# Second mixture of experts: routing work spread over eleven rounds of first products instead of one, with its data in a pool of its own

## The chip, the cores and the metric

The kernel runs on one core of a Trainium2 chip. The time is the device time of one execution in microseconds (us). TensorE (PE in the profile) multiplies matrices, its weight loads are listed as PEld; VectorE is DVE, ScalarE is ACT, GpSimd is POOL, and SyncE (SP) issues most of the DMA transfers. Each engine works through its own list of instructions in order.

## The reference, cut to what matters

The program is a stack of blocks over x of 256 tokens by 1024 columns in fp32. The part that is changed is the feed-forward stage of the second block of the second network (the "second mixture"): a mixture of 8 experts, of which each token takes two, with d_ff 2816.

```python
def moe_swiglu(x, router_w, router_b, w1, w3, w2):
    logits = (x @ router_w + router_b).astype(jnp.float32)
    top_v, top_i = lax.top_k(logits, TOP_K)          # TOP_K = 2
    top_p = jax.nn.softmax(top_v, axis=-1)
    gate = jnp.sum(jax.nn.one_hot(top_i, N_EXPERTS_2, dtype=jnp.float32) * top_p[..., None], axis=-2)
    out = jnp.zeros_like(x)
    for e in range(N_EXPERTS_2):                     # 8
        out = out + gate[..., e:e + 1] * swiglu(x, w1[e], w3[e], w2[e])
    return out
```

Around it stand an RMS norm of x before (its gain is g_ffn), the addition of the result to x, and afterwards a gated projection and a last norm.

## The kernel before, in words

**Stages.** The program runs through the phases b1, moe1, mix0, ffn0, ple0, mix1, ffn1, ple1 and fin. The second mixture is ffn1, and lies between about 1400 and 2105 us.

**Weights.** All weights of the mixture come as 264 blocks of 1 MB (128 x 2048 fp32), fetched by one queue on SP (class `Stream`, line 236; the transfer is issued in line 264). It has nine slots in this phase, three that all phases share and six more. A slot is given back when the next block is asked for (`get`), so SP waits until the products that read it are done, then issues the next transfer, strictly in the order of use.

**Blocks.** The 8 experts go in two groups c of four. A group has eleven rounds j of first products (gate and up columns), each of 8 blocks (k, one for each 128 of the 1024 columns), so 88 blocks, and then two down products d of 22 blocks. `tiles` (line 1918) does one block: eight products on quarters of the PE array (32 columns each, printed 128*32, tiles u = 0 to 7), whose weights are gathered tokens and which go to PSUM banks r0 and r1; three copies by ScalarE of a part of the block, chosen at run time, into `fw` (line 314, two buffers, FLEX = 2; these are called flex copies here); and six narrower products from `fw` into the third bank. After the 8 blocks of a round, the hand-over: ScalarE takes Silu of the three banks (line 303, `ft<-ps`), VectorE multiplies into `ft`, and, during block 2 of the next round (`flush` at k == 2), transposes `ft` into `hT` (line 2093), the input of the down products. Blocks are counted here from 0 through the whole phase: round j starts at block 8j, and the second group at block 132.

**Routing.** A token's place within its expert turns into a one-hot matrix P (tokens x slots), per group 640 columns: 256 "base" columns, 64 slots for each of the four experts (`base`), and 384 "strip" columns, 12 strips of 32 for the experts with more tokens (`fewest` finds which have the fewest, `strips` spreads the places by six copies into px, `more` compares them with a ramp). From P come:

- the gathers (`gathered`, line 1069): 8 steps per group, one for each 128 columns, four full-width products each (ps<-P,htmh and ps<-P,html, 352 columns); even steps are evicted into xg by VectorE, odd ones by ScalarE;
- the slot sums (`of_slots`, line 1088): one-column products ps<-rs,P that give each slot its token's norm factor (rsl), which Silu and the product after it use as scale;
- the shares (`shares`, line 958): Wt, the two gates of a token, by Exp on ScalarE, then `strips` of it;
- twelve rounds of transposes of P into pt (ps<-c,P, line 233; two or three at a time) with four sets of five share products (ps<-c,Pw) whose sums become wsl; pt and wsl are used after the down products;
- the flag (`over_flag`): whether an expert has more tokens than slots.

**Order.** The order of TensorE, ScalarE and VectorE is that in which the program writes the instructions. The generator `rest()` holds all routing of the second group and what follows; `beside` puts it in a list and each `tick` runs it to its next `yield`; `drain` runs it to its end. In the kernel before, `during(k)` stands ahead of each of the 8 blocks of the first round: two further steps of the first gather, the slot sums at k == 2, `rest()` from k == 3 on with three ticks per block; `drain` follows. The pool m2r that holds P, the places and so on is closed after that round, and m2e (hT, yf, four ft buffers) opens in its place; xs, the overflow's input, is a view of a part of hT that is not yet filled.

**Overflow test.** After round 5 of the first group all engines read the flag (`values_load` of fi) and branch; with these inputs no expert overflows and the branch only skips. The changed lines are 1936 to 2130.

Of the kernel before, what the change touches and what calls it, by code (L numbers as in the profile page):

```python
# [7 lines left out]
F32 = mybir.dt.float32  # L8
F32R = mybir.dt.float32r
# [3 lines left out]
ALU = mybir.AluOpType  # L13
# [3 lines left out]
D, S = 1024, 256  # L17
# [8 lines left out]
CAP1, CAP2 = 32, 64  # L26
# [251 lines left out]
class Kern:  # L278
# [1615 lines left out]
    def moe2(self, x):  # L1894
# [13 lines left out]
        with tc.tile_pool(reuse_waits="tile", name="m2", bufs=1) as pool:  # L1908
# [27 lines left out]
            with tc.tile_pool(reuse_waits="tile", name="m2r", bufs=1) as rt:  # L1936
# [30 lines left out]
                def strips(src, name):  # L1967

                    s, o = four(src), rt.tile([128, 2, 2, 3, 4], F32, name=name)
                    d = rt.tile([128, 2, 2, 3], F32, name=name + "d")  # L1970
                    nc.vector.tensor_sub(d, s[:, :, :, 1:4], s[:, :, :, 0:3])
                    nc.vector.tensor_tensor(d, d, mk[:, None].to_broadcast([128, 2, 2, 3]), op=ALU.mult)
                    nc.vector.tensor_add(d, d, s[:, :, :, 0:3])
                    for i in range(3):
                        n = 3 - i
                        nc.vector.tensor_copy(o[:, :, :, i, :n], d[:, :, :, :n])
                        nc.vector.tensor_copy(o[:, :, :, i, n:], d[:, :, :, n - 1:])
                    return o.rearrange("p t c i g -> p t c (i g)")
# [9 lines left out]
                def rest():  # L1988
                    with self.after((nc.cur_bb, self.first)):
                        base(1)  # L1990
                    more(1)
# [3 lines left out]
                    wx = strips(Wt, "wx")  # L1995
                    bw = self.bank()
                    for t in range(2):
                        for c in range(2):
                            for r0, r1 in ((0, 3), (3, 5)):
                                b = self.bank()  # L2000
                                for r in range(r0, r1):
# [5 lines left out]
                            Pw = rt.tile([128, L], F32, name="Pw")  # L2007
                            Pc = P[:, t, L * c:L * c + L].bitcast(F32)
                            nc.vector.tensor_tensor(v3(Pw[:, :B], CAP2), v3(Pc[:, :B], CAP2), bc(Wt[:, t, 4 * c:4 * c + 4], CAP2),
                                                    op=ALU.mult)  # L2010
                            nc.vector.tensor_tensor(v3(Pw[:, B:], 32), v3(Pc[:, B:], 32), bc(wx[:, t, c], 32), op=ALU.mult)
                            for r in range(5):
                                bw.mm(bw.t[:, 5 * c + r:5 * c + r + 1], Pw[:, 128 * r:128 * r + 128], self.cst("ones")[:, 0:1])
# [35 lines left out]
            m13 = self.A["m13"].rearrange("q j k p e d -> q j k p e d")  # L2049
            m2 = self.A["m2"].rearrange("q f (j c) p e d -> q f j c p e d", c=2)  # L2050

            def units(first, unit):
                with tc.For_i(0, 2, 1) as q:
                    first()
                    with tc.For_i(0, 11, 1) as j:
                        for e in range(4):
                            unit((q, j, e), e)
            one = lambda i: bass.ds(i, 1)
            with tc.tile_pool(reuse_waits="tile", name="m2e", bufs=1) as work:
                hT = work.tile([128, 22, R], F32, name="hT")  # L2060
                yf = [work.tile([128, 512], F32R, name="yf" + n) for n in "hl"]
                for y in yf:
                    nc.vector.tensor_scalar(y, iota[:, None, :].to_broadcast([128, 4, 128]), 0.0, None, op0=ALU.mult)

                xs = hT[:, 16:].rearrange("p a r -> p (a r)")[:, :8 * S].rearrange("p (k s) -> p k s", k=8)
                later = []

                def flush():
                    while later:
                        later.pop(0)()  # L2070

                for c in range(2):
                    for j in range(11):
                        g = g0 if c == j == 0 else first_products(c, lambda k: flush() if k == 2 else None)
                        ts = []
                        for r in range(3):
                            t = work.tile([128, 256], F32, name="ft", bufs=4)
# [19 lines left out]
                        if c == 0 and j == 5:  # L2097
# [3 lines left out]
                                          lambda v: v.rearrange("p (q a i d) -> p q a i d", q=4, a=2, i=2))  # L2101
                    if c:

                        self.raw = self.parts = self.split(F32R)
                    for d in range(2):
# [6 lines left out]
                        ys = [[work.tile([128, 512], F32R, name="y" + n, bufs=2) for n in "hl"] for _ in range(2)] + [yf]  # L2112
# [60 lines left out]
```

## Time and profile before

| What | Value |
|---|---|
| Time, median of 3 runs | 2163.77 us (2163.45 to 2166.29) |
| Profiled execution | 2167.51 us, with a span of 2165.9 us |
| Mean granted clock of PE | 0.976 of full speed |
| PE busy | 2016.7 us, 93% |
| PEld busy | 1461.7 us, 67% |
| VectorE busy | 1060.6 us, 49% |
| ScalarE busy | 1080.2 us, 50% |
| GpSimd busy | 18.7 us, 1% |
| DMA | 613.73 MB, mean 283 GB/s |

The profiled execution is one run, recorded by the hardware; the span goes from its first to its last instruction. Busy time is the time in which an instruction of the engine was under way; weight loads of PE overlap with its products. In the timelines a row is one instruction or a row of like ones (xcount), with the time at which the first began, and in brackets how long the engine idled before and what ended that.

### The profile page before, as it was taken

The page shows a single profiled execution, that of the slowest core. Times are in us where ns is not written, and L with a number is a line of the kernel's source. Part 1 is how long each engine was busy: PE and PEld are TensorE (multiplying, and loading weights), DVE is VectorE, ACT ScalarE, POOL GpSimd, SP SyncE. Part 2 cuts the span into 40 slices and gives each one's busy share as a digit, 9 for nine tenths or more (in the row PEclk, how much of TensorE's full clock was granted, in tenths as well). Part 3 has the DMA queues.
Part 4 walks back from the last instruction along what each step waited for, and adds up shares of the span by engine and source line. Part 5 has one row for each costly group of instructions (what it writes and reads, how often), then busy time and mean ns, then how long its engine had stood idle before and what let it go on. Part 6 is the DMA issues. An engine that isn't in the chain of part 4 may idle for free. (4 is left out here: it accounts for less than half of the span.)

```text
span 2165.9 us, 44126 instructions
## 1 busy us (share of the span) xinstructions
PE 2016.7 (93%) x17740; PEld 1461.7 (67%) x17740; DVE 1060.6 (49%) x2809; ACT 1080.2 (50%) x2178; POOL 18.7 (1%) x29
## 2 busy tenths in 40 slices
PE   7999998787877779999999999999899999999997
PEld 6999994222222248879999888866566756666746
DVE  5787653100100037777666787536655115566115
ACT  5566642000000025456456735457677777777775
POOL 0000000000000010000000100000000000000000
PEclk9999999899999999999999999889999999999998
DMA  5344597999999983316555331449999999999981
GB/s 179 120 146 149 175 376 305 418 420 420 419 420 420 419 343 109 109 61 216 179 193 191 114 128 52 175 159 396 399 410 418 416 405 407 418 418 417 418 351 47
DMA packets 88665, 613.73 MB, mean 283 GB/s; under 512 B 9879, under 2 KB 12071, under 8 KB 18560
## 3 DMA queue, kind: packets, MB, share of 16 engines
q1 hardware_dynamic: 86272, 604.74, 71.1%
q0 software_dynamic: 1344, 5.10, 0.7%
q8 instruction: 143, 2.34, 0.4%
q10 hardware_dynamic: 832, 0.94, 0.1%
q14 instruction: 74, 0.61, 0.1%
HBM read 609.69 MB, written 1.05 MB: 282 GB/s over the span
## 5 line engine op out<-in xcount | busy, mean ns | idle before, releaser
L314 ACT COPY fw<-w 128x512 f32 x792 | 439.0, 617 | 137.3 <-ACT fw L314 91.9
L341 ACT CAST wh<-w 128x512 fp32r<-128x512 f32 (+2 forms) x500 | 289.8, 585 | 293.8 <-PE ps L230 247.1
L342 DVE TENSOR_TENSOR wl<-w,wh 128x512 fp32r<-128x512 f32 (+2 forms) x500 | 317.9, 646 | 169.9 <-ACT wh L341 161.8
L230 PE MATMUL ps<-w,hT 128*32 128x512 f32 x1920 | 311.0, 597 | 31.4 <-DMA w<-wdn 26.0
L230 PE MATMUL ps<-rawh,wh 128*128 128x256 f32 x960 | 277.4, 289 | 1.1 <-ACT rawh L341 1.1
L230 PE MATMUL ps<-rawl,wh 128*128 128x256 f32 x960 | 271.0, 282 | 0.5 <-DVE rawl L342 0.5
L230 PE MATMUL ps<-rawh,wl 128*128 128x256 f32 x960 | 270.5, 282 | 0.0
L230 PE MATMUL ps<-fw,xg 128*32 128x384 f32 (+2 forms) x2112 | 252.8, 382 | 0.0
L230 PE MATMUL ps<-w,xg 128*32 128x512 f32 x1024 | 199.5, 600 | 43.2 <-DMA w<-wgu 43.0
L2093 DVE STREAM_TRANSPOSE hT<-ft 32x64 f32<-32x64 f32 x968 | 228.3, 236 | 16.3 <-DVEq L985 0.7
L230 PE MATMUL ps<-w,rawh 128*32 128x512 f32 x1408 | 206.2, 607 | 6.4 <-issue 6.4
L230 PE MATMUL ps<-w,rawl 128*32 128x512 f32 x1408 | 211.7, 593 | 0.0
L230 PEld LDWEIGHTS ps<-w,hT 128*32 128x32 f32 x1920 | 116.8, 110 | 135.6 <-DMA w<-wdn 64.0
L230 PEld LDWEIGHTS ps<-fw,xg 128*32 128x32 f32 x2112 | 137.8, 110 | 83.0 <-issue 24.0
L230 PEld LDWEIGHTS ps<-rawh,wh 128*128 128x128 f32 x960 | 181.8, 190 | 5.1 <-ACT rawh L341 1.6
L230 PEld LDWEIGHTS ps<-rawl,wh 128*128 128x128 f32 x960 | 181.9, 190 | 1.9 <-DVE rawl L342 0.7
L230 PEld LDWEIGHTS ps<-rawh,wl 128*128 128x128 f32 x960 | 181.9, 189 | 1.5 <-issue 0.9
L230 PEld LDWEIGHTS ps<-w,xg 128*32 128x32 f32 x1024 | 42.1, 109 | 185.7 <-DMA w<-wgu 111.7
L230 PEld LDWEIGHTS ps<-w,rawl 128*32 128x32 f32 x1408 | 105.2, 110 | 34.4 <-issue 0.9
L230 PE MATMUL ps<-hh,wh 128*128 128x256 f32 x416 | 124.4, 300 | 0.1
L230 PE MATMUL ps<-fw,hT 128*32 128x128 f32 (+2 forms) x1056 | 121.1, 380 | 0.5 <-ACT fw L314 0.3
L230 PE MATMUL ps<-hh,wl 128*128 128x256 f32 x416 | 116.2, 281 | 0.2 <-DVE wl L342 0.2
(520 smaller groups left out, 2983.7 us busy)
## 6 DMA issues: line engine op xcount, KB each, us to landing
w<-m SPq DMA_DIRECT2D x264, 1024.0 KB, 10.7
w<-wgu SPq DMA_DIRECT2D x128, 1024.0 KB, 19.9
w<-wdn SPq DMA_DIRECT2D x64, 1024.0 KB, 19.9
w<-f SPq DMA_DIRECT2D x32, 1024.0 KB, 5.1
w<-wz SPq DMA_DIRECT2D x20, 1024.0 KB, 5.5
w<-wdh SPq DMA_DIRECT2D x24, 768.0 KB, 4.3
w<-wb SPq DMA_DIRECT2D x16, 1024.0 KB, 5.6
w<-wo SPq DMA_DIRECT2D x8, 1024.0 KB, 5.1
```

The source lines that it names most:

```text
L230: return self.k.nc.tensor.matmul(out, lhsT, rhs, start=new, stop=stop, skip_group_check=True, **kw)
L314: self.nc.scalar.copy(out, in_)
L341: self.nc.scalar.copy(h, src)
L342: self.nc.vector.tensor_sub(l, src, h.bitcast(F32))
L2093: nc.vector.transpose(hT[32 * f:32 * f + 32, 2 * j:2 * j + 2, o:o + 32], ts[r][32 * s:32 * s + 32, 64 * q:64 * q + 64].rearrange("p (i d) ...
```

## The change: what it does

The routing of the first group keeps its beginning, but with less ahead of the first gather: `strips` is split in two (`thirds`, three VectorE instructions, and `strips`, the six copies), and `more` gets the places and an offset, so that only the first 96 strip columns, one per third, are made before the first gather; the six copies and the other 288 columns are written at k == 5 of the first round. The slot sums of the first group and `rest()` start at k == 7 instead of 2 and 3.

`rest()` then goes on beside the following rounds: `beside(k)` stands ahead of every later block, and steps it once at each odd k, so four times per round, and `yield`s stand between its pieces as before (one more ahead of its gathers). The drain, the closing of the routing's pool and the overflow test follow after round 10 of the first group instead of after round 0 and round 5. For this the routing's pool m2r lies on the other side ("right") of the on-chip memory, hT and ft are in m2e from the start, ft has three buffers instead of four, xs has a pool of its own, yf and ys are in a new pool on the right after the test, and the weighted P (Pw) uses a temporary tile ("rsy") in two pieces. The computation is the same.

```diff
@@ the pools
-            with tc.tile_pool(reuse_waits="tile", name="m2r", bufs=1) as rt:
+            right = lambda name: tc.tile_pool(reuse_waits="tile", name=name, bufs=1, side="right")
+            with ExitStack() as routing, tc.tile_pool(reuse_waits="tile", name="m2e", bufs=1) as work:
+                rt = routing.enter_context(right("m2r"))
...
-                def strips(src, name):
+                def thirds(src, name):
-                    s, o = four(src), rt.tile([128, 2, 2, 3, 4], F32, name=name)
-                    d = rt.tile([128, 2, 2, 3], F32, name=name + "d")
+                    s, d = four(src), rt.tile([128, 2, 2, 3], F32, name=name)
                     nc.vector.tensor_sub(d, s[:, :, :, 1:4], s[:, :, :, 0:3])
                     nc.vector.tensor_tensor(d, d, mk[:, None].to_broadcast([128, 2, 2, 3]), op=ALU.mult)
                     nc.vector.tensor_add(d, d, s[:, :, :, 0:3])
+                    return d
+                def strips(d, name):
+                    o = rt.tile([128, 2, 2, 3, 4], F32, name=name)
...
-                def more(c):
+                def more(c, places, a):
                     for t in range(2):
-                        nc.vector.tensor_tensor(v3(P[:, t, L * c + B:L * c + L], 32), bc(psx[:, t, c], 32),
-                                                iota[:, None, CAP2:CAP2 + 32].to_broadcast([128, 12, 32]), op=ALU.is_equal)
+                        o = v3(P[:, t, L * c + B + a:L * c + B + a + 32 * places.shape[-1]], 32)
+                        nc.vector.tensor_tensor(o, bc(places[:, t, c], 32), iota[:, None, CAP2:CAP2 + 32].to_broadcast(
+                            [128, places.shape[-1], 32]), op=ALU.is_equal)
...
                 def rest():
                     with self.after((nc.cur_bb, self.first)):
                         base(1)
-                    more(1)
+                    more(1, f["px"], 0)
+                    yield
                     yield from gather(1)
...
                 f = {}
+                fewest()
+                pst = thirds(ps, "pd")
                 base(0)
-                fewest()
-                psx = strips(ps, "px")
-                more(0)
+                more(0, pst, 0)
...
                 def during(k):
                     for _ in range(2):
                         next(start, None)
-                    if k == 2:
+                    if k == 5:
+                        f["px"] = strips(pst, "px")
+                        more(0, f["px"][:, :, :, 3:], 96)
+                    if k == 7:
                         self.of_slots(rsl[:, :5], P[:, :, :L], rs)
-                    if k == 3:
                         self.beside(rest(), late=True)
-                    for _ in range(3):
-                        self.tick()
-                g0 = first_products(0, during)
-                self.drain()
...
+                def beside(k):
+                    if k == 2:
+                        flush()
+                    if k % 2:
+                        self.tick()
...
                 for c in range(2):
                     for j in range(11):
-                        g = g0 if c == j == 0 else first_products(c, lambda k: flush() if k == 2 else None)
+                        g = first_products(c, beside if c or j else during)
                         ts = []
                         for r in range(3):
-                            t = work.tile([128, 256], F32, name="ft", bufs=4)
+                            t = work.tile([128, 256], F32, name="ft", bufs=3)
...
-                        if c == 0 and j == 5:
+                    if not c:
+                        self.drain()
+                        routing.close()
+                        with right("m2o") as room:
+                            xs = room.tile([128, 8, S], F32, name="xs")
                             self.overflow(pool, x, ("g_ffn1", xs, lambda: None), rk, *f["over"], E, units,
...
+                        outs = routing.enter_context(right("m2y"))
+                        yf = [outs.tile([128, 512], F32R, name="yf" + n) for n in "hl"]
```

TensorE round the slot sums of the second group, in the kernel before. Here `ps<-P,html` is the last gather product of the group, `ps<-rs,P` a slot sum, `ps<-c,P` a transpose into pt, `w,rawh` and `fw,xg` the products of one block (the latter from the flex copies):

```order
L230 MATMUL ps<-P,html 128x352
L230 MATMUL ps<-rs,P 128x1 x10
L233 MATMUL ps<-c_78,P 128x128 x3
L230 MATMUL ps<-w,rawh 32x512 x8
L230 MATMUL ps<-fw,xg_13969 32x384
L230 MATMUL ps<-fw,xg_13969 32x128
L230 MATMUL ps<-fw,xg_13969 32x256
L230 MATMUL ps<-fw,xg_13969 32x384
L230 MATMUL ps<-fw,xg_13969 32x256
L230 MATMUL ps<-fw,xg_13969 32x128
L233 MATMUL ps<-c_78,P 128x128 x2
```

The gather's last steps, the slot sums, and the transposes come one right behind the other, and the next pieces of the routing follow after each single block. The same place in the changed order, which is now inside the fourth round of first products, after block 27:

```order
L230 MATMUL ps<-fw,xg_13969 32x128
L230 MATMUL ps<-rs,P 128x1 x10
L233 MATMUL ps<-c_78,P 128x128 x3
L230 MATMUL ps<-w,rawh 32x512 x8
L230 MATMUL ps<-fw,xg_13969 32x384
L230 MATMUL ps<-fw,xg_13969 32x128
L230 MATMUL ps<-fw,xg_13969 32x256
L230 MATMUL ps<-fw,xg_13969 32x384
L230 MATMUL ps<-fw,xg_13969 32x256
L230 MATMUL ps<-fw,xg_13969 32x128
L230 MATMUL ps<-w,rawh 32x512 x8
```

The gather's last step now stands two blocks earlier, by itself; the slot sums and three transposes stand between two blocks, and two blocks follow each other before the next piece.

ScalarE in the kernel before, at the end of the first round, with the first Silu (`ft<-ps,rsl`) and the flex copies (`fw<-w`); `pt<-ps` evicts transposes, and ISA belongs to the flex copies, whose source is chosen at run time:

```order
L314 CAST pt<-ps 128x2x128
L314 CAST pt<-ps 128x3x128
L314 CAST pt<-ps 128x2x128
L314 ISA
L314 COPY fw<-w 128x512
L303 ACT_TABLE_LOAD
L303 ACTIVATE ft<-ps,rsl 128x256 x2
L303 ACTIVATE ft<-ps,rsl 128x64
L314 ISA
L314 COPY fw<-w 128x512
```

All casts into pt and the flex copies up to the first hand-over's stand before the first table load; after it only Silu and flex copies follow. ScalarE in the changed order, at a hand-over near the end of the second group's gathers (`rawl<-ps,pv` and `xg<-ps,pv` evict a gather step):

```order
L303 ACTIVATE ft<-ps,rsl 128x64
L314 ISA
L314 COPY fw<-w 128x512
L303 ACTIVATE ft<-ps,rsl 128x64
L295 ACT_TABLE_LOAD
L301 ACTIVATE rawl<-ps,pv 128x256
L301 ACTIVATE xg_13970<-ps,pv 128x96
L314 ISA
L314 COPY fw<-w 128x512
L314 ISA
```

The gather's evictions now stand between Silus and flex copies, with a load of another table before them (line 295, for the Exp of the shares); the casts into pt and the Exp of the shares follow later, between the rounds.

## Rows read from the trace of the kernel before

**Rows 1.** The chain that ended last, shares of the span by engine.
```profile
PE 26%; ACT 1%; DVE 1%; issue 0%; DVEq 0%; ACTq 0%
```

**Rows 2.** Busy us: PE, PEld, DVE, ACT, POOL; granted clock, DMA share, GB/s.
```profile
1409.30:1460.20 50.90, 50.86 (x409) 32.49 (x412) 14.37 (x52) 25.66 (x57) 0.00 (x0) 0.89 0.48 167
1460.20:1550.00 89.80, 89.80 (x1068) 58.66 (x1065) 59.88 (x243) 68.25 (x136) 0.00 (x0) 1.00 0.99 398
```

**Rows 3.** Waits from 1413 to 2106 us: total, number, longest.
```profile
PE ps L230 <- issue: 6.4, 1, 6.4
SPq L264 <- PE ps L230: 598.9, 227, 21.9
```

**Rows 4.** Weight transfers of line 264 between 1460 and 1700 us.
```profile
DMA to landing us min/median/max: 5.2/10.0/15.6
```

**Rows 5.** PE timeline, first products of four blocks: start, us, operation.
```profile
1476.80 0.60 PE L230 MATMUL ps<-w,rawh 128*32 128x512 f32 x1
1479.16 0.60 PE L230 MATMUL ps<-w,rawh 128*32 128x512 f32 x1
1599.65 0.59 PE L230 MATMUL ps<-w,rawh 128*32 128x512 f32 x1
1602.65 0.62 PE L230 MATMUL ps<-w,rawh 128*32 128x512 f32 x1
```

**Rows 6.** Timeline of VectorE and PE before the first gather.
```profile
1408.08 0.15 DVE L1976 COPY px<-pxd 128x12 f32<-128x12 f32 x1
1408.66 1.95 DVE L1982 TENSOR_TENSOR P<-px,c 128x384 fp32r<-128x384 f32 x4
1409.34 0.63 PE L230 MATMUL ps<-P,htmh 128*128 128x352 f32 x1 [3.41 <-DVE P L1982]
```

**Rows 7.** PE timeline, the routing among the first blocks.
```profile
1417.35 1.92 PE L230 MATMUL ps<-w,rawh 128*32 128x512 f32 x16
1419.09 0.83 PE L230 MATMUL ps<-fw,xg 128*32 128x384 f32 x12
1419.85 0.43 PE L230 MATMUL ps<-P,htmh 128*128 128x352 f32 x1
1420.11 0.32 PE L230 MATMUL ps<-P,html 128*128 128x352 f32 x1
1420.27 0.32 PE L230 MATMUL ps<-P,htmh 128*128 128x352 f32 x1
1421.22 2.29 PE L230 MATMUL ps<-rs,P 128*128 128x1 f32 x20
1423.44 3.24 PE L230 MATMUL ps<-w,rawh 128*32 128x512 f32 x16
1426.43 1.27 PE L230 MATMUL ps<-fw,xg 128*32 128x384 f32 x12
...
1441.99 3.08 PE L230 MATMUL ps<-w,rawh 128*32 128x512 f32 x16
```

**Rows 8.** Busy time, the 10 us round the first slot sums.
```profile
1420.00:1430.00 10.00, 10.00 (x71) 7.29 (x72) 2.25 (x7) 4.41 (x11) 0.00 (x0) 0.83 0.51 175
```

**Rows 9.** Timeline of ScalarE and PE's weight loads at hand-overs.
```profile
1457.35 1.28 ACT L303 ACT_TABLE_LOAD   x1
1458.64 1.04 ACT L303 ACTIVATE ft<-ps,rsl 128x256 f32<-128x256 f32 x3
...
1465.86 1.66 ACT L314 COPY fw<-w 128x512 f32 x3 [0.70 <-ACT fw L314]
...
1602.62 0.12 PEld L230 LDWEIGHTS ps<-fw,xg 128*32 128x32 f32 x3 [0.38 <-ACT fw L314]
```

**Rows 10.** PE timeline at the overflow test.
```profile
1559.76 3.64 PE L230 MATMUL ps<-w,rawh 128*32 128x512 f32 x16 [6.44 <-issue]
1564.14 1.91 PE L230 MATMUL ps<-w,rawh 128*32 128x512 f32 x16
```

**Rows 11.** VectorE timeline, the transposes into hT after a hand-over.
```profile
1464.40 7.78 DVE L2093 STREAM_TRANSPOSE hT<-ft 32x64 f32<-32x64 f32 x31
```

More of the change, by code (lines that the diff above doesn't have):

```diff
@@ L1994, in rest @@
                     Wt = self.shares(rt, oh1, oh2, v1, v2, E)
-                    wx = strips(Wt, "wx")
+                    wx = strips(thirds(Wt, "wd"), "wx")
                     bw = self.bank()
@@ L2006, in rest @@
                                 yield
-                            Pw = rt.tile([128, L], F32, name="Pw")
                             Pc = P[:, t, L * c:L * c + L].bitcast(F32)
[L2009 to L2013, printed above, removed]
+                            for r0, n, col in ((0, CAP2, Wt[:, t, 4 * c:4 * c + 4]), (2, 32, wx[:, t, c])):
+                                m = n * col.shape[-1]
+                                Pw = self.tmp.tile([128, 512], F32, name="rsy")[:, :m]
+                                nc.vector.tensor_tensor(v3(Pw, n), v3(Pc[:, 128 * r0:128 * r0 + m], n), bc(col, n), op=ALU.mult)
+                                for r in range(m // 128):
+                                    bw.mm(bw.t[:, 5 * c + r0 + r:5 * c + r0 + r + 1], Pw[:, 128 * r:128 * r + 128],
+                                          self.cst("ones")[:, 0:1])
                             yield
@@ L2040, in during @@
                         next(start, None)
-                    if k == 2:
+                    if k == 5:
+                        f["px"] = strips(pst, "px")
+                        more(0, f["px"][:, :, :, 3:], 96)
+                    if k == 7:
                         self.of_slots(rsl[:, :5], P[:, :, :L], rs)
-                    if k == 3:
                         self.beside(rest(), late=True)
-                    for _ in range(3):
-                        self.tick()
-                g0 = first_products(0, during)
-                self.drain()
[L2049 to L2059, printed above, removed]
                 hT = work.tile([128, 22, R], F32, name="hT")
[L2061 to L2065, printed above, removed]
                 later = []
@@ L2070, in flush, with units @@
                         later.pop(0)()
+                def beside(k):
[3 more added lines that the diff above has]
+                        self.tick()
+                m13 = self.A["m13"]
+                m2 = self.A["m2"].rearrange("q f (j c) p e d -> q f j c p e d", c=2)
+                def units(first, unit):
+                    with tc.For_i(0, 2, 1) as q:
+                        first()
+                        with tc.For_i(0, 11, 1) as j:
+                            for e in range(4):
+                                unit((q, j, e), e)
+                one = lambda i: bass.ds(i, 1)
                 for c in range(2):
                     for j in range(11):
-                        g = g0 if c == j == 0 else first_products(c, lambda k: flush() if k == 2 else None)
+                        g = first_products(c, beside if c or j else during)
                         ts = []
                         for r in range(3):
-                            t = work.tile([128, 256], F32, name="ft", bufs=4)
+                            t = work.tile([128, 256], F32, name="ft", bufs=3)
                             gu = g[r].t.rearrange("p (q a d) -> p q a d", a=2, d=64)
@@ L2101, in moe2 @@
                                           lambda v: v.rearrange("p (q a i d) -> p q a i d", q=4, a=2, i=2))
+                        outs = routing.enter_context(right("m2y"))
+                        yf = [outs.tile([128, 512], F32R, name="yf" + n) for n in "hl"]
+                        for y in yf:
+                            nc.vector.tensor_scalar(y, iota[:, None, :].to_broadcast([128, 4, 128]), 0.0, None, op0=ALU.mult)
                     if c:
@@ L2111, in moe2 @@
                                 flush()
-                        ys = [[work.tile([128, 512], F32R, name="y" + n, bufs=2) for n in "hl"] for _ in range(2)] + [yf]
+                        ys = [[outs.tile([128, 512], F32R, name="y" + n, bufs=2) for n in "hl"] for _ in range(2)] + [yf]
                         for r in range(3):
```

## The prediction

> **What bounds the kernel now.** I read the page first (times by engine, then the chain that ended last), then busy time by stretch, then the waits of TensorE and of the weight queue inside the second mixture, and last the instructions in order of time around its routing.
>
> The page offers two suspects. The chain that ended last is TensorE for 26% of the span, some 560 us, with the other engines at 1% or less [rows 1]: it is followed back to 1560 us, into the second mixture, and lies on TensorE nearly all that way. But the table by stretch shows the DMA share at 0.99 and 398 GB/s there as well (1460 to 1550 us), after a stretch from 1409.3 to 1460.2 us in which DMA is at 0.48 and 167 GB/s [rows 2]. That stretch is the routing: TensorE alternates eight blocks of the first products with gathers, slot sums, transposes and share products. If weights were late, the empty stretch would be worth filling. The waits say who is late: from 1413 to 2106 us TensorE's only long wait is one of 6.4 us with no releaser, and no DMA releases it at all, while the queue that issues weights waits 598.9 us for TensorE [rows 3]. Issue to landing is at most 15.6 us between 1460 and 1700 us [rows 4], and nine slots at 2.36 us a block (1476.80 to 1479.16 [rows 5]) are 21 us. DMA looks full because TensorE frees one slot after another, just about as fast as they can be filled. So in this mixture TensorE's own time sets the end, and moving its work along its in-order queue gains only what it idles or wastes now.
>
> **The change, term by term.** I compare with the profiled execution (2167.51 us), which is 3.74 us above the median 2163.77 of the runs shown.
>
> 1. *Head.* The first gather waits 3.41 us for P [rows 6]. VectorE now makes only 96 of the 384 strip columns first, and the six copies into px come after them. The copies start at 1408.08 and the strips at 1408.66 [rows 6]; one of four strip products is 1.95 / 4 = 0.49, and a quarter as wide I take 0.2. That is 0.4 to 0.6 for the copies and the share product between, 0.3 for the narrower strip: **-0.7** (0 to -0.9). ScalarE now evicts a gather before the first flex copies; those are needed only when the wide products of block 0 are through, so I count nothing.
>
> 2. *Breaks.* Every piece of the routing remains (the same gathers, slot sums, transposes, share products, flag), so their raw times cancel. What changes is how often TensorE leaves the 32-column products for full-width ones. Now the pieces stand in 9 gaps, after blocks 0 to 8; in the new order they stand in 25: after blocks 0, 1, 2 and 6, eight single gathers on every second block, then slot sums with three transposes, eleven gaps of two or three transposes or five share products, and the flag. One gap costs: a block alone takes 2.50 (1417.35 to 1419.85 [rows 7]) against 2.36 in a run [rows 5], 0.13 or so; the first gather product takes 0.26 to its successor (1419.85 to 1420.11) where the next takes 0.16 (to 1420.27), 0.10; and the way back 0.10. So a gather gap has 0.33 of waste, a gap of transposes or share products 0.13 to 0.23. Eight more gather gaps at 0.33 are 2.6; eight other ones at 0.13 are 1.0: **+3.6**. Bounds: 16 x 0.10 = 1.6 and 16 x 0.33 = 5.3.
>
> The rows show the loss at each change of width. [...]
>
> 3. *Half clock.* Both runs of slot sums (ps<-rs,P, 2.2 us of one-column products, 1421.22 to 1423.44) are followed by a block at 3.24 and 3.08 instead of 1.92 [rows 7]; the granted clock is 0.83 in the 10 us round the first [rows 8], where the dense stretch has 1.00 [rows 2]: part of it at 1.2 GHz, the rest at 2.4. The first cost (3.24 + 1.27) - (1.92 + 0.83) = 1.76, the second 1.16, together 2.9. In the new order the slot sums stand alone amid dense blocks. The trace does not show such a place. Both ends: both remain (0), both vanish (-2.9). I take one of two, **-1.4**.
>
> 4. *ScalarE's order.* A block needs three flex copies, 1.66 of each 2.36, so ScalarE has 0.70 to spare [rows 9]. At the hand-over to the next first products its Silus stand among them. Where copies go first nothing is lost (2.36 [rows 5]); where all three copies of a block stand behind the first Silus, TensorE waits for fw and the block starts 3.00 after the one before (1599.65 to 1602.65 [rows 5, 9]): 0.64. That happens now at four hand-overs of the first group, after the overflow test. In the new order the first three are clean, four are late as now (to blocks 56 to 80), two (to 32 and 48) half late, 0.5 each. Also two more ACT_TABLE_LOADs stand there, since the exponential's set is asked for after Silu: 1.28 each [rows 9]. One comes before the last gather eviction and a block's copies, beyond the 0.70: 0.5; the other stands in idle time before a Silu. **+1.5** (0 to +4.2).
>
> 5. *The overflow test* moves from the middle of the first products to their end. It costs 6.44 idle and a first block that takes 4.38 instead of 2.36 (1559.76 to 1564.14 [rows 10]), 8.5. TensorE idles although nothing holds it, so I let it cost the same at the new place: **0** (-0.6, as it swallows a late hand-over, to +0.8). Its flag stands after block 49 in the new order, some 38 x 2.36 = 90 us before the test, and the weight queue reads it without a wait.
>
> 6. *Elsewhere.* hT from the start, xs in a room of its own and three ft buffers instead of four: the transposes of a block group are through 12 us after its hand-over (the last run starts at 1464.40 and takes 7.78 [rows 11]), the next Silus come after 19 us, so no wait. Between the first group's two down products TensorE's order shifts by one block: **0** (-1 to +1). The second group stands as it was.
>
> Sum: -0.7 + 3.6 - 1.4 + 1.5 = **+3.0**: 2170.5 for the profiled execution, less 3.74: **2166.8 us**.
>
> **Rivals.**
>
> *B, the queue decides.* If weights bound the mixture, the routing beside later blocks would start the transfers earlier. Blocks 0 to 8 take 50.9 us now instead of 9 x 2.36 = 21.2; some 7 us of gaps stay before block 8, so up to 22 us could come free: 2142. For it: DMA share 0.99 [rows 2]. Against it: no wait of TensorE on DMA [rows 3]. Chance 0.05.
>
> *C, ScalarE is late* (the slower side). The new order puts four gather evictions, eight pt casts and two table loads among the flex copies. It decides as soon as what stands before a block's copies exceeds the 0.70 to spare, at a place where TensorE has only the two fw buffers. Price at the worst: late at all of the hand-overs to blocks 8 to 48 (6 x 0.64 = 3.8) and both table loads in full (2.6), 6.4 in place of my 1.5: +7.9, 2171.7. Against it: most of these stand where a gather also holds TensorE up. Chance 0.25. [...]
>
> *D, breaks are cheap and the clock stays up.* The pieces are short, so full-width products might slip in at the low bound (+1.6) and the slot sums might no longer pull the clock down (-2.9): -0.7 + 1.6 - 2.9 + 1.5 = -0.5, 2163.3; without ScalarE's 1.5 also 2161.8. Against it: 2.50 at every lone block. Chance 0.20.
>
> **How the numbers follow.** About 0.2%, 4.3 us, is what a measurement here tells from no change. My case has 0.50, of which 0.08 lies above +4.3. Slower: 0.25 + 0.08 = 0.33. Faster: B's 0.05 and 0.04 of D: 0.09. Same: 0.58. The range goes from D's end to C's, about 1 further on each side for the spread of the runs shown (2163.45 to 2166.29): 2160.8 to 2173.0.
>
> **What would show it.** Right: from the first gather to the overflow test no wait of TensorE on DMA, single gathers each with some 0.97 between two blocks (0.33 of waste, 0.64 of products); the test's 6.4 us again, now after block 87; block spacing 2.36 afterwards. Term 3 is right if one of the two stretches at 1.2 GHz after ps<-rs,P is gone. Term 4 shows as idle weight loads released by fw copies at the hand-overs to blocks 32 and 48 and after the added table load. Wrong: any TensorE wait on w<-m (then the queue does count), a test that costs much less than 8.5, or blocks that keep 2.36 beside lone gathers.

## The result, and the profile after

| | median us | runs | ratio to the kernel before, 95% interval |
|---|---|---|---|
| Kernel before | 2163.61 | 4 (2163.38 to 2166.29) | |
| Changed kernel | 2177.20 | 4 (2173.42 to 2178.29) | 1.0057 [1.0039, 1.0074] |
| Changed kernel again (first experiment) | 2173.60 | 10, beside 27 of before at 2165.59 | 1.0039 [1.0023, 1.0055] |

The change makes the kernel slower by 8 to 14 us; 2166.8 was predicted, with a range up to 2173.0. Executions of one and the same kernel lie up to 10.7 us from their median, and the slower ones have the lower mean clock (of the kernel before, beside e12: 0.982 at 2156.83 us, 0.974 at 2170.97; TensorE spends 82 to 111 us at half clock in the profiles below), so kernels are compared by their ratios, and places by the blocks' start times. Half clock is a granted clock of 0.50 instead of 1.00, for which the prediction has 1.2 and 2.4 GHz: in the kernel before it is 0.50 from 1403.5 to 1413.5 us, where gather products of 352 columns start every 0.29 us (an estimated 1.2 columns per ns), from 1424.0 to 1427.3 and from 1441.1 to 1444.3. The profiled execution after took 2173.42 us, with a span of 2171.8, 5.9 more than before.

Where it lies is read from the start times of the 264 blocks' first products in the two timelines:

| Stretch | before, us | after, us | difference |
|---|---|---|---|
| start of block 0 | 1413.1 | 1412.1 | -1.0 |
| block 0 to 47 | 137.03 | 137.81 | +0.8 |
| 47 to 50 (test of before, one gap of after) | 16.34 | 8.47 | -7.9 |
| 50 to 87 | 89.44 | 89.59 | +0.1 |
| 87 to 90 (test of after) | 7.74 | 21.85 | +14.1 |
| 90 to 116 | 68.04 | 67.46 | -0.6 |
| 116 to the end | 434.2 | 434.5 | +0.3 |

In this profile all that is lost is lost at the overflow test: the two rows with a test make +6.2 together, and the others come to less than half a microsecond the other way. The waits of TensorE and of the weight queue from 1412 to 2112 us, as in [rows 3] (total, number, longest):

```profile
PE ps L230 <- DMA w<-m: 12.4, 1, 12.4
PE ps L230 <- ACT yfh L301: 1.6, 2, 1.2
...
SPq L264 <- PE ps L230: 601.1, 226, 22.4
```

The one wait of 6.4 is now one of 12.4. It is put down to a weight transfer, wrongly: that block's transfer had landed 20 us before its first product (1643.4 against 1663.6). TensorE's timeline at the test, which answers to [rows 10]:

```profile
1649.93 1.19 PE L230 MATMUL ps<-fw,xg 128*32 128x256 f32 x11
1663.56 3.49 PE L230 MATMUL ps<-w,hT 128*32 128x512 f32 x16 [12.43 <-DMA w<-m]
1666.81 0.88 PE L230 MATMUL ps<-fw,hT 128*32 128x384 f32 x12
1667.46 1.95 PE L230 MATMUL ps<-w,hT 128*32 128x512 f32 x16
```

The test's branches (line 985: durations in ns, then first and last start in us) and VectorE's timeline:

```profile
L985 PEldq COMPARE_BRANCH  x2: 75/3020/5965, 1648.9 to 1651.3; - x2
...
L985 DVEq COMPARE_BRANCH  x2: 47/54/61, 1662.4 to 1663.4; - x2
```

```profile
1651.42 0.22 DVE L2103 STREAM_TRANSPOSE hT<-ft 32x64 f32<-32x64 f32 x1
...
1651.86 1.48 DVE L2103 STREAM_TRANSPOSE hT<-ft 32x64 f32<-32x64 f32 x6
...
1653.68 1.99 DVE L2103 STREAM_TRANSPOSE hT<-ft 32x64 f32<-32x64 f32 x8
...
1656.02 7.23 DVE L2103 STREAM_TRANSPOSE hT<-ft 32x64 f32<-32x64 f32 x29
1663.91 0.43 DVE L2120 TENSOR_SCALAR yfh<-c 128x512 fp32r<-128x512 f32 x1 [0.67 <-DVEq L985]
```

TensorE's own branch takes the same 5.97 us and is through at 1657.3. VectorE has all 44 transposes of the last round ahead of its read of the flag, passes the test at 1663.4, and TensorE goes on at 1663.5 with a weight load and at 1663.56 with a product. In the kernel before 16 of them stood ahead and 28 behind (below, VectorE's last rows round its branch); VectorE passed at 1558.5, a microsecond ahead of TensorE:

```profile
L985 PEldq COMPARE_BRANCH  x2: 75/3022/5968, 1551.2 to 1553.5; - x2
...
L985 DVEq COMPARE_BRANCH  x2: 47/54/61, 1557.5 to 1558.5; - x2
```

```profile
1552.90 0.48 DVE L2093 STREAM_TRANSPOSE hT<-ft 32x64 f32<-32x64 f32 x2
...
1553.93 0.23 DVE L2093 STREAM_TRANSPOSE hT<-ft 32x64 f32<-32x64 f32 x1
...
1554.51 0.98 DVE L2093 STREAM_TRANSPOSE hT<-ft 32x64 f32<-32x64 f32 x4
...
1555.84 1.99 DVE L2093 STREAM_TRANSPOSE hT<-ft 32x64 f32<-32x64 f32 x8
...
1558.17 0.24 DVE L2093 STREAM_TRANSPOSE hT<-ft 32x64 f32<-32x64 f32 x1
1559.08 7.00 DVE L2093 STREAM_TRANSPOSE hT<-ft 32x64 f32<-32x64 f32 x28 [0.67 <-DVEq L985]
```

So the description of the kernel before is wrong in one point: VectorE's order is not that of the program's text. In the text the transposes of a round belong to block 2 of the next round, or to block 1 of the down products, which is behind the test in both kernels. When the program is built, its instructions are put in order once more, and in the traces the transposes begin as soon as a part of `ft` is ready.

The routing's own rows, as in [rows 6] and [rows 7] (PE timeline: first gather, first slot sums, a lone gather between two blocks):

```profile
1408.31 0.63 PE L230 MATMUL ps<-P,htmh 128*128 128x352 f32 x1 [2.53 <-DVE P L1990]
...
1433.98 2.39 PE L230 MATMUL ps<-rs,P 128*128 128x1 f32 x20
1436.31 1.92 PE L230 MATMUL ps<-w,rawh 128*32 128x512 f32 x16
...
1443.42 1.91 PE L230 MATMUL ps<-w,rawh 128*32 128x512 f32 x16
1445.13 0.84 PE L230 MATMUL ps<-fw,xg 128*32 128x384 f32 x12
1445.90 0.43 PE L230 MATMUL ps<-P,htmh 128*128 128x352 f32 x1
...
1446.75 1.92 PE L230 MATMUL ps<-w,rawh 128*32 128x512 f32 x16
```

The first gather waits 2.53 instead of 3.41; the block behind the slot sums takes 1.92, not 3.24; and a lone gather costs 3.33 - 2.36 = 0.97.

### The profile page after: what moved, and what is told of

The parts are those of the page before. It is cut to its first block, busy times and chain, and to the rows that moved or that the text cites. A ratio compares the mean times of both kernels' runs of the same rounds, so it can differ in the third digit from the quotient of the medians.

```text
span 2171.8 us, 44140 instructions
## 1 busy us (share of the span) xinstructions
PE 2018.6 (93%) x17740; PEld 1433.1 (66%) x17740; DVE 1061.3 (49%) x2811; ACT 1082.0 (50%) x2180; POOL 18.6 (1%) x29
## 3 DMA queue, kind: packets, MB, share of 16 engines
q8 instruction: 144, 2.36, 0.4%
## 4 chain that ended last, share of the span: by engine, by line
PE 74%; DMA 20%; ACT 3%; DVE 2%; issue 1%; DVEq 0%; ACTq 0%; SPq 0%; POOLq 0%
PE ps L230 72%; DMA w<-wgu 13%; DMA w<-wdn 7%; PE ps L233 1%; DMA w<-m 1%; DVE wl L342 0%; ACT fw L314 0%; ACT wh L341 0%; ACT yfh L301 0%; DMA sm<-sm 0%; ACT mt L301 0%; ACT L303 0%; DVE yfl L2144 0%; ACT yh L301 0%; ACT L295 0%
## 5 line engine op out<-in xcount | busy, mean ns | idle before, releaser
L230 PE MATMUL ps<-w,hT 128*32 128x512 f32 x1920 | 303.0, 601 | 43.5 <-DMA w<-wdn 25.6
L2103 DVE STREAM_TRANSPOSE hT<-ft 32x64 f32<-32x64 f32 x968 | 228.5, 236 | 15.2
L230 PE MATMUL ps<-fw,xg 128*32 128x384 f32 (+2 forms) x2112 | 229.1, 380 | 0.0
L230 PEld LDWEIGHTS ps<-w,hT 128*32 128x32 f32 x1920 | 105.6, 110 | 155.9 <-issue 69.1
L230 PE MATMUL ps<-w,rawh 128*32 128x512 f32 x1408 | 184.9, 597 | 0.0
L230 PEld LDWEIGHTS ps<-fw,xg 128*32 128x32 f32 x2112 | 125.0, 110 | 84.1 <-issue 23.9
L230 PE MATMUL ps<-hl,wh 128*128 128x256 f32 x416 | 116.0, 279 | 0.0
```

Source lines behind the costliest of these rows:

```text
L230: return self.k.nc.tensor.matmul(out, lhsT, rhs, start=new, stop=stop, skip_group_check=True, **kw)
L2103: nc.vector.transpose(hT[32 * f:32 * f + 32, 2 * j:2 * j + 2, o:o + 32], ts[r][32 * s:32 * s + 32, 64 * q:64 * q + 64].rearrange("p (i d) ...
```

## The experiments

"Loss at the test" is what the three blocks from it on take beyond 2.36 each (47 to 50, 63 to 66 or 87 to 90); the stretch is from the first block's start to the last one's; both from the profile.

| Kernel | median us (of before beside it) | ratio, 95% interval | stretch | loss at the test |
|---|---|---|---|---|
| before | | | 690.8 | 9.3 |
| changed | 2177.2 (2163.6) | 1.0057 [1.0039, 1.0074] | 697.2 | 14.8 |
| e1 changed again | 2173.6 (2165.6) | 1.0039 [1.0023, 1.0055] | 698.3 | 15.1 |
| e2 transposes behind the test | 2172.5 (2165.6) | 1.0035 [1.0020, 1.0051] | 697.7 | 13.8 |
| e3 test after round 7 | 2172.1 (2165.6) | 1.0030 [1.0017, 1.0044] | 696.7 | 15.2 |
| e4 before, test after round 10 | 2172.8 (2165.6) | 1.0032 [1.0020, 1.0044] | 696.3 | 13.6 |
| e5 changed, no test | 2159.0 (2166.2) | 0.9971 [0.9957, 0.9984] | 684.3 | |
| e6 before, no test | 2159.3 (2166.2) | 0.9975 [0.9964, 0.9986] | 686.6 | |
| e7 e2, landing shifted | 2165.5 (2166.2) | 1.0000 [0.9987, 1.0014] | 692.4 | 10.1 |
| e8 e4, landing shifted | 2168.6 (2166.2) | 1.0015 [1.0003, 1.0027] | 690.2 | 10.2 |
| e9 before, short body | 2164.6 (2166.2) | 0.9996 [0.9985, 1.0008] | 690.7 | 8.9 |
| e10 e2, short body | 2161.4 (2166.2) | 0.9974 [0.9962, 0.9986] | 687.9 | 4.8 |
| e11 before, all of it | 2160.9 (2167.6) | 0.9976 [0.9962, 0.9990] | 686.1 | 6.0 |
| e12 e11, slot sums later | 2163.0 (2167.6) | 0.9983 [0.9965, 1.0000] | 686.8 | 5.8 |

**e1**, no edit. 

> The changed kernel once more, beside the kernel before on the same chip. Four timed runs gave 2173.4 to 2178.3 us, and the one profiled was the fastest: span 2171.8, clock 0.976; the others had spans of 2174.9 to 2176.7 and clocks of 0.973 to 0.974. Theory T (the overflow test): of the 13.6 us about 6.2 lie at the test, where TensorE stands still 12.4 us instead of 6.4 and VectorE has 44 transposes of the last round ahead of its own read of the flag; that part is in every profile. Theory C (clock): the other 3 to 5 us are stretches at half clock somewhere in the spread routing, so a profile at 2176 to 2178 shows one or two more of them between 1410 and 1550 us than the first profile (none). Expected median 2176 to 2178.

The median came out below the 2176 to 2178 that were expected. The loss at the test is there again (15.1). One stretch at half clock follows the first slot sums (none in the first profile): the block behind them takes 4.08 instead of 2.39. Theory C stays open for the rest: the first four runs are slower than these ten, at a mean clock of 0.974 against 0.977, and no profile shows where.

**e2**

```diff
-                                flush()
+                                with self.after(None if c or d else (nc.cur_bb, cleared)):   # cleared: the zeroing of yf
+                                    flush()
```

> The changed kernel, but the transposes of the last round of the first group are held back behind the test (behind the clearing of yf), so VectorE reads the flag at once. Theory T: TensorE idles some 6.4 us at the test, its first down block starts some 6 us sooner, and the median is 5 to 6.5 below the changed kernel's (about 2171). Rival L (the place itself: the jump over the overflow's code is longer in coming at the end of the group, or the first down product waits for weights): no gain, within 1 us of the changed kernel.

The first part of T holds and the gain does not come. TensorE's timeline:

```profile
1650.78 1.93 PE L230 MATMUL ps<-w,hT 128*32 128x512 f32 x6 [6.60 <-DVE hT L2103]
1656.18 2.72 PE L230 MATMUL ps<-w,hT 128*32 128x512 f32 x9 [3.47 <-issue]
```

It begins 6.6 us after its stop, runs 6 of 16 products, and stands a second time for no releaser. In the changed kernel such a stop would lie hidden under VectorE's: the transfer that ends it (see e4) began at 1660.7 there, and VectorE held TensorE until 1663.4.

**e3**

```diff
-                    if not c:
+                        if c == 0 and j == 7:
                             self.drain()
                             ...
```

> The changed kernel, but the drain, the closing of the routing's pool, the test and the pool of yf stand after round 7 of the first group instead of round 10 (the flag is made in round 6). VectorE still has its 44 transposes ahead of its read of the flag, but behind the test TensorE goes on with first products, which read xg and not hT. Theory T: TensorE waits 6.4 there, median 5 to 6.5 below the changed kernel's (about 2171). If it is VectorE's late branch by itself that holds TensorE, and not hT: no gain.

```profile
1606.62 3.64 PE L230 MATMUL ps<-w,rawh 128*32 128x512 f32 x16 [12.47 <-DVEq L985]
```

No gain: behind the test stand first products that read no hT, and they wait 12.47 us until VectorE's branch (DVEq L985) all the same. So T was wrong in one word: it is not the data that TensorE waits for but VectorE's passing of the test.

**e4**

```diff
-                        if c == 0 and j == 5:
+                        if c == 0 and j == 10:
-                xs = hT[:, 16:]...
+                xs = work.tile([128, 8, S], F32, name="xs")
```

> The kernel before with one edit: the test after round 10 of the first group instead of round 5, and xs in a tile of its own. In the order of this kernel 16 transposes of the last round stand ahead of VectorE's read of the flag and 28 behind it. Theory T: VectorE is through about when TensorE is, so 0 to 2 above the kernel before (2164 to 2166). Rival L (the place itself): some 6 above it (2170).

The test is moved (and xs with it), and the kernel before loses about as much as by the whole change (1.0032 against 1.0039). T alone does not say so, since VectorE is through in time here (its branch begins at 1655.3):

```profile
1656.49 1.89 PE L230 MATMUL ps<-w,hT 128*32 128x512 f32 x2 [6.48 <-issue]
1662.02 2.78 PE L230 MATMUL ps<-w,hT 128*32 128x512 f32 x11 [3.64 <-issue]
```

Two products, then the second stop. Beside it stand the transfers of queue q8 (of the kind `instruction` on the page: 144 of 16 KB, for 35,480 products and weight loads of TensorE, from which I estimate about 250 instructions each):

```
        transfers behind the jump, us   TensorE goes on   second stop
before  1557.0  1563.0                  1559.8            none
changed 1654.8  1660.7                  1663.6 (VectorE)  none
e2      1647.9  1653.7                  1650.8            until 1656.2
e4      1653.6  1659.4                  1656.5            until 1662.0
e7      1651.4  1656.9                  1654.1            none
e8      1649.5  1655.2                  1652.2            none
```

Where VectorE lets it, TensorE goes on 2.4 to 2.9 us after a transfer has begun, and the next one comes 5.5 to 6 us after the first. Counted in the built programs, the jump of e4 lands 8 instructions further into its piece than that of e2, and e4 runs four products (8 instructions) fewer before it stops: both stop at the same place, taken here to be the end of the piece that was fetched (some 16 instructions on in e2, 8 in e4). That end is my estimate from the stops and transfers of these two runs; no trace shows where a piece ends. Whether the second stop hangs on the place of the landing was tried in e7 and e8.

**e7, e8**: the same edit in e2 and in e4, inside the part that is jumped over.

```diff
             for t in range(2):
-                b.tr(b.t[:n, 128 * t:128 * t + 128], wo[:, t], self.cst("ident"))
+                for _ in range(11 if keep == "g_ffn1" else 1):
+                    b.tr(b.t[:n, 128 * t:128 * t + 128], wo[:, t], self.cst("ident"))
```

> The kernel e2 (last transposes behind the test) with 20 more transposes of TensorE inside the guarded part, which is jumped over: they only move the place where TensorE's instructions go on by some 40 instructions. In e2 TensorE began the first down block 6.6 us after it stopped, ran 6 products, and stood again from 1652.6 to 1656.2 us, until 2.4 us after the next 16 KB transfer of the instruction queue had begun (1653.7). Theory F (instruction fetch: the jump landed a few instructions ahead of the end of a fetched piece): the second stop is gone, the blocks 88 to 90 lose 9 to 10 instead of 13.8, from first to last block 4 us less than e2 (697.7), median 3 to 5 less. Rival: the second stop comes from something else (hT, ScalarE's copies): nothing changes.

> The kernel e4 (the kernel before with its test after round 10) with the same 20 transposes inside the guarded part. In e4 TensorE ran two products of the first down block and stood from 1658.4 to 1662.0 us, until 2.6 us after the next 16 KB instruction transfer had begun (1659.4). Theory F: the second stop is gone, from first to last block 691 to 692 us instead of 696.3, median within 1.5 of the kernel before. Rival: as e4.

```profile
1654.12 3.64 PE L230 MATMUL ps<-w,hT 128*32 128x512 f32 x16 [6.51 <-DVE hT L2104]
1657.50 1.54 PE L230 MATMUL ps<-fw,hT 128*32 128x384 f32 x12
1658.78 2.35 PE L230 MATMUL ps<-w,hT 128*32 128x512 f32 x16
```

Forty instructions that never run take the second stop away in both (e7 above: all 16 products in one row): 13.8 becomes 10.1, 13.6 becomes 10.2. With VectorE out of the way and a good landing the changed order costs what the kernel before costs (1.0000). e8's median stays a little above (1.0015, where 1.5 us at most were expected), though its stretch is as short as that of the kernel before; no profile shows where.

**e5, e6**

```diff
-                            self.overflow(pool, x, ("g_ffn1", xs, lambda: None), rk, *f["over"], E, units,
...
```

> The changed kernel without the second mixture's overflow test and what it guards (a part of the computation that these inputs never enter). Theory T2: all that the change lost lies at the test, where TensorE waits until VectorE has passed it too (VectorE has 44 transposes ahead of it), and where its instructions behind the jump must be fetched again. From the first block to the last of the mixture: the profile's 697 to 698 us less 13 to 14.5, so about 683.5; median 12 to 15 below the changed kernel's (about 2160 where the kernel before has 2165). Rival S (the spread routing costs several us by itself): this kernel is 3 us or more above the kernel before without its test.

> The kernel before without the second mixture's overflow test (the same part left out). From the first block to the last of the mixture 690.8 less 9 (7.2 of idle and 2.0 of half clock), about 681.7; median some 9 below the kernel before (about 2156). Theory T2: the kernel e5 stands 0 to 3 above this one, breaks and lost half-clock stretches about cancelling; rival S: 4 or more above.

Without the test the two orders cannot be told apart (0.9971 and 0.9975, intervals overlapping), which is T2's side. But e6's stretch is 686.6, not 681.7, and its median is 7 us below, not 9: two hand-overs that the test had swallowed are late (1.2), and blocks 90 to 110 take 49.6 us where before they took 47.2. So part of what the spread routing costs by itself (some 2 us up to block 50, see below) is hidden in this comparison. The waits from 1640 to 1698 us, and two blocks there:

```profile
ACT fw L314 <- DMA w<-m: 14.9, 16, 2.4
...
PEld ps L230 <- DMA w<-m: 2.0, 10, 0.3
```

```profile
1671.09 1.92 PE L230 MATMUL ps<-w,hT 128*32 128x512 f32 x16
1672.83 0.86 PE L230 MATMUL ps<-fw,hT 128*32 128x384 f32 x12
1673.58 1.92 PE L230 MATMUL ps<-w,hT 128*32 128x512 f32 x16
```

ScalarE's copies wait for weights, and a block takes 2.49: 1 MB at the 418 GB/s of that stretch is 2.51. This is rival B's mechanism. The kernel before uses a block every 2.36 in the same blocks; the test, which is all that e6 leaves out, gave the queue a pause in which to fill its slots.

**e9, e10**: the four experts of the guarded part as a run-time loop.

```diff
                 with tc.For_i(0, 2, 1) as q:
-                    first()
-                    with tc.For_i(0, 11, 1) as j:
-                        for e in range(4):
-                            unit((q, j, e), e)
+                    with tc.For_i(0, 4, 1) as e:
+                        first()
+                        with tc.For_i(0, 11, 1) as j:
+                            unit((q, j, e), 0)
...
```

> The kernel before, with the guarded part made shorter: the four experts of a group are a run-time loop instead of being written out four times, so TensorE's jump over it goes over 295 instructions instead of 868, some 1.2 pieces of 16 KB instead of 3.4 (this part is never entered with these inputs). At the test TensorE's branch took 5.97 us there, ScalarE's and VectorE's, over a few dozen to a hundred, 0.04 to 0.05. Theory F1 (what costs is that the target has not been fetched yet, and the next piece is fetched ahead): the branch takes well under 2 us, block 48 loses 1 to 3 instead of 7.2 and block 49 no half clock, median 5 to 9 below the kernel before. Theory F2 (each long jump fetches anew): 6 us as before, and since it lands some 20 instructions ahead of the end of a piece, a second stop as in e2 and e4, median about 4 above the kernel before.

> The kernel e2 (the changed kernel with its last transposes behind the test) with the same shorter guarded part; TensorE's jump goes over 295 instructions and lands 77 ahead of the end of a piece. F1: block 88 loses 1 to 3, block 89 nothing: from first to last block 685 to 687 us instead of e2's 697.7, median 5 to 9 below the kernel before. F2: the branch takes 6 us, then a second stop of some 1 to 3 us once the 77 instructions (1.4 blocks) are through: 694 to 696, median 2 to 5 above the kernel before.

The branches and TensorE's timeline of e10:

```profile
L985 PEldq COMPARE_BRANCH  x2: 63/228/393, 1646.3 to 1648.8; - x2
```

```profile
1651.12 3.37 PE L230 MATMUL ps<-w,hT 128*32 128x512 f32 x16 [2.51 <-DVEq L985]
1654.30 0.83 PE L230 MATMUL ps<-fw,hT 128*32 128x384 f32 x12
```

F1 for the jump: over 295 instructions it takes 0.39 us (0.31 in e9), over 868 it took 5.97; what is fetched ahead, the traces do not show. What is left in e10 is VectorE with its five products of the hand-over, and half clock. The gain of e10 is just short of the 5 us at least that were expected (4.8). In e9 the expected gain does not come, for TensorE still stands 5.4 us:

```profile
1555.93 3.64 PE L230 MATMUL ps<-w,rawh 128*32 128x512 f32 x16 [5.41 <-ACT fw L314]
```

Its own branch is through at 1551.1. ScalarE's copies end at 1555.79, and VectorE, with 16 transposes ahead of it, begins its branch at 1555.76; the trace doesn't tell the two apart. So a short jump alone is worth nothing (0.9996), as a free VectorE alone was (e2).

**e11, e12**: e9 with round 5's transposes held behind the test and the narrow first strips; then with the slot sums moved.

```diff
e11
-                more(0)
+                more(0, pst, 0)
...
+                            held = later.pop()
+                            with self.after((nc.cur_bb, nc.vector.memset(ec[0:1], 0.0))):
+                                held()
e12
-                    if k == 2:
+                    if k == 7:
                         self.of_slots(rsl[:, :5], P[:, :, :L], rs)
```

> The kernel before with what the runs point to: the shorter guarded part (e9), the transposes of round 5 held behind the test, and of the change only the narrow first strips (96 columns ahead of the first gather, the other 288 at k == 1). In e9 the branch took 0.3 us but TensorE still lost 6.2 + 2.3 + 0.4 at blocks 48 to 50, waiting for VectorE with 16 transposes ahead of its own branch. Theories T2 and F1 together: blocks 48 to 50 lose 4 to 5.5 as in e10 (3.3 + 1.5), the first gather comes 0.7 to 1.0 us sooner, so 4 to 6 below e9 and the kernel before, median about 2160 to 2162 where the kernel before has 2166. If holding the transposes back only moves the wait (to ScalarE's Silus, or VectorE's products): within 2 of the kernel before.

> The kernel e11 with the slot sums of the first group at k == 7 instead of k == 2 (behind block 6, as in the changed kernel, but amid the transposes and share products of before). In the kernel before each of the two runs of slot sums is followed by 3.4 us at half clock (2.9 us together), in the changed kernel's seven profiles so far the first one is in four, the second in none. Theory C (slot sums between gathers pull the clock down, amid blocks they do so half the time): one of the two stretches goes in some executions, 0 to 1.5 below e11. Rival: they do so wherever they stand amid other one-column products: within 0.5 of e11.

e11 beats both kernels, as e10 does. A second stop of 2.44 us is left: behind this short jump too the landing is near the estimated end of a piece (some 21 instructions ahead, counted as for e2 and e4), and TensorE goes on 2.5 us after the next transfer has begun (1552.9):

```profile
1551.56 1.45 PE L230 MATMUL ps<-w,rawh 128*32 128x512 f32 x9 [2.64 <-DVEq L985]
1555.46 0.63 PE L230 MATMUL ps<-w,rawh 128*32 128x512 f32 x4 [2.44 <-issue]
```

e12 is inconclusive: it is not told from e11, and both profiles have one stretch at half clock in the routing where the kernel before has two. e8, whose routing is that of the kernel before, has one as well, so a stretch less is no sign of an edit.

## Why the prediction was wrong

*The bound* was right: TensorE's own time, and no wait for weights; the queue waits 601 us for it.

*Step 1, head*: -0.7 said, 3.41 - 2.53 = -0.9 measured.

*Step 2, breaks*: right to the hundredth for a lone gather (0.97). From block 0 to 50 the changed kernel takes 146.28, the kernel before 153.37 less its test's 9.27, 144.10: +2.2. The half clock went (-2.9) and block 0 lay deeper in a stretch at half clock (4.98 instead of 4.21), which leaves some 4.3 for the breaks; 3.6 was said.

*Step 3, half clock*: -1.4 said, as the middle of two ends; in the profile after both stretches are gone (-2.9), which is partly luck. In the seven profiles of the changed order the second one never comes and the first one in four.

*Step 4, ScalarE*: +1.5 said, nothing measured. Up to block 48 every gap has its plain size; only blocks 65, 73 and 81 start 0.63 late, as before. The two table loads (at 1487.67 and 1506.20, 1.28 each) are hidden.

*Step 5, the overflow test, is the step that failed*: "TensorE idles although nothing holds it, so I let it cost the same at the new place: 0". It lost 14.8 instead of 9.3 in the profile, +5.5, or +4.8 with the late hand-over that it swallows at the new place (21.85 - 7.74 = 14.1), and more than the whole change was said to cost. All other terms together made +1.1 where +3.0 was said. TensorE goes on only when VectorE has passed too: in the changed kernel, e1 and e3 its first product begins 0.18 us after VectorE's second branch does, when its own has been through for some 6 us. And 44 transposes stand ahead of VectorE's read instead of 16. Had they not been there, the jump's new landing, some 16 instructions ahead of the second stop, would have cost nearly as much (13.8 in e2, 13.6 in e4), which e7 shows by shifting it (10.1). "Nothing holds it" was wrong for the kernel before as well: of its 6.44 us TensorE spends 5.97 in its own branch, which the list of waits shows only as `issue`. The order of VectorE's instructions round the test could have been read beforehand, and step 6 even had the 12 us that they take after a hand-over; I read the engine that idled, not those that it must meet there.

*Step 6, elsewhere*: 0 said, -0.6 between blocks 90 and 116.

*Rivals*: B has its mechanism (e6), but not in these two kernels; its price was too high, since the 50.9 us hold 3.8 us of the first gather as well. C and D were both off, ScalarE not late and the breaks not cheap. No rival had the test, and the only sign of being wrong that was named for it was that it costs less. Of the 8 to 14 us measured, the profile shows 5.9. The ratios put the 8 of e1 at the test: it costs the changed kernel 0.68% (1.0039 less 0.9971, e5), some 15 us, and the kernel before 0.25% (e6), some 5, since there the weights take a part back. The further 5 to 6 us of the first four runs go with their lower clocks, and their place stays open.

## What to carry to other kernels

A branch in the middle of a program can be a meeting of engines, as it is here for TensorE and VectorE (in three kernels TensorE's first product begins 0.18 us after VectorE's second branch): before moving one, read for each engine what stands ahead of its own branch at the new place, for here the last one set the time. TensorE's jump itself cost 5.97 us over 868 instructions and 0.39 over 295, and its landing a second stop of 3.47 in e2 and none in e7: keep guarded code short (a loop instead of four copies took 6 us to 0.4), and look for idle time of TensorE with no releaser just behind a jump. When a pause is taken away, see whether it had been what kept a queue ahead: e6 gave 2.4 of the 9.3 us back to the weights up to block 110, and 1.3 more behind block 116, where TensorE itself waits 1.2 us for one.

## What the runs showed of the hardware that was not expected

- TensorE's jump over 868 instructions (908 in e7 and e8) takes 5.92 to 6.22 us in eight kernels (5.97 in the kernel before and the changed one, 6.10 in e2) and 0.31 to 0.39 us over 295 in four (0.39 in e10); ScalarE's and VectorE's, over a hundred or fewer, take 0.03 to 0.06.
- Behind the long jump the second 16 KB transfer of q8 begins 5.5 to 6 us after the first (4.0 in e3). In e4 and e2, by estimate 8 and 16 instructions behind the landing, TensorE stood again for 3.5 to 3.6 us, until 2.4 to 2.6 us after that second transfer had begun; 40 unexecuted instructions removed that. Behind the short jump it stood again for 2.4, an estimated 21 behind the landing (e11).
- When the weights limit the mixture, a block takes 2.49 us (e6); otherwise it takes 2.36. So the lead of nine slots shrinks, and in e6, without the test's pause, it is used up after some 95 blocks.
